# FFN raw tiles: four made and zeroed once per layer, instead of one GpSimd memset for each use

## The chip, the cores and the metric

The kernel runs on one core of one Trainium2 chip. The metric is device time in microseconds of one execution, as the median of several runs; lower is better. TensorE (PE in the profile) multiplies, VectorE (DVE), ScalarE (ACT) and GpSimd (POOL) do elementwise work, SyncE (SP) issues most transfers. PEld is the loading of weights into TensorE, which runs beside its matmuls.

## The reference, cut to what matters

Two layers, each a token mixer and then a gated convolutional FFN. The change lies in the FFN, which runs twice:

```
D_MODEL = 1024; SEQ = 1024; D_FF = 2816; FFN_CONV = 3

def causal_dwconv(x, w, b):
    k_width = w.shape[0]
    s = x.shape[1]
    xp = jnp.pad(x, ((0, 0), (k_width - 1, 0), (0, 0)))
    y = b
    for k in range(k_width):
        y = y + w[k] * xp[:, k:k + s]
    return y

def conv_ffn(xn, up_w, conv_w, conv_b, down_w):
    h = causal_dwconv(xn @ up_w, conv_w, conv_b)
    g, u = h[..., :D_FF], h[..., D_FF:]
    return (jax.nn.silu(g) * u) @ down_w
```

The convolution looks two tokens back, so each channel's sequence begins with zeros (`jnp.pad`).

## The kernel before, in words

Activations lie with channels on the 128 partitions and the 1024 tokens along the free axis, in two halves of 512. Every product is made in three passes on numbers that are split into a high part (a rounded copy, made by a cast on ScalarE) and a low part (what is left, made by a subtraction on GpSimd): high by high, high by low, low by high. So each weight block costs a cast `wh<-...` on ScalarE, then a subtraction `wl<-...` on GpSimd, and the third pass of each product cannot begin before that subtraction has ended.

`ffn_layer` makes 22 pairs of channel blocks (gate and value). Pairs 0 and 1 are made by plain products. Pairs 2 to 21 go through one loop (from line 968), an iteration each, which makes a 2 by 2 block product with seven half-size products in place of eight (a Winograd form), so that each iteration first needs sums of the weights: `sums` (lines 935 to 943, VectorE) writes the tiles `sa` and `sc` from the weight tiles `ws`. The products of an iteration are, in TensorE's order, `px` and `py` (weights from `ws`), `px` again and `pz` (from `sa`), `px` again (from `sc`, with the operand `t3h`), `pw` (from `a22h`), `pz` again (from `sc`): 84 matmuls of 512 columns. The third use of `px` adds on top of the second, after a ScalarE copy (line 979) has saved what stood there.

The results are gathered in raw tiles of 1028 columns: four columns in front, of which the last two are the zeros that the convolution looks back on, then the 1024 tokens. `new_raw` (lines 822 to 825) takes one from a pool of four buffers and zeroes the four columns on GpSimd. An iteration takes two (`lo` and `hi`), and `conv` (lines 834 to 847) reads them: on ScalarE the last tap (line 839), on VectorE the other two taps (line 841, two passes for each of the two tiles, four in a row), then the gate (silu, line 844, ScalarE), the product of gate and value (line 846, VectorE) and the store to `a_d`. The convolution of one iteration runs during the next one.

A layer of the language puts each engine's instructions into an order of its own and derives the waits; a buffer of a pool is given out again when the last reader of its old content is done. The memset of a buffer is therefore an instruction in GpSimd's queue that waits for VectorE. The functions that the change touches:

Of the kernel before, what the change touches and what calls it, by code (L numbers as in the profile page):

```python
# [9 lines left out]
F32 = mybir.dt.float32  # L10
# [8 lines left out]
P = 128  # L19
T = 1024  # L20
# [46 lines left out]
def trunk_kernel(ctx: ExitStack, tc: tile.TileContext, a: dict, stages=None):  # L67
    nc = tc.nc
    pe, act, dve, pool, sp = nc.tensor, nc.scalar, nc.vector, nc.gpsimd, nc.sync
# [733 lines left out]
    def ffn_layer(i, final_store, next_gain):  # L803
# [6 lines left out]
        sb = st.enter_context(tc.tile_pool(name=f"ffu{i}", bufs=2, reuse_waits="tile"))  # L810
# [8 lines left out]
        HB = KB // 2  # L819
        W2 = HB * P  # L820

        def new_raw():
            raw = sb.tile([P, T + 4], F32, name="raw", tag="raw", bufs=4)
            pool.memset(raw[:, 0:4], 0.0)
            return raw

        def half(raw, h):
            return raw[:, 4 + h * HT:4 + (h + 1) * HT]
# [53 lines left out]
        def load_pair(j):  # L882
# [6 lines left out]
            return {"ws": ws}  # L889

        raws = [new_raw() for _ in range(2 * PLAIN)]
        plain = [(h, n) for h in range(2) for n in range(2 * PLAIN)]
        w = split_weight(a["ffn_up_w"][i, 0], KB, 1)
# [73 lines left out]
        for j in range(PLAIN, PAIRS):  # L967
            end = j == PAIRS - 1
            nxt = None if end else load_pair(j + 1)
            lo, hi = new_raw(), new_raw()  # L970
            px, py = ps_a([P, HT], "px"), ps_b([P, HT], "py")
            pz, pw = (ups.tile([P, HT], F32, name=f"p{c}", tag=c) for c in "zw")
# [559 lines left out]
    for idx, s in enumerate(stages):  # L1532
        last = idx == len(stages) - 1
        ng = None if last else first_gain[stages[idx + 1]]
        if s == "ssd":
            ssd_layer(begin, ng if ng is not None else gffn[:, 0], prepare if "attn" in stages else (lambda: None))
        elif s in ("ffn0", "ffn1"):
            dst = a["out"] if last else x_d
            ffn_layer(int(s[-1]), dst, ng)
            src = dst  # L1540
        else:
            attn_layer(tabs["attn"], src, ng if ng is not None else gffn[:, 1])
        if last and not s.startswith("ffn"):
            for h in range(2):
                for m in range(KB):
                    store_x(a["out"], m, h)
# [87 lines left out]
```

## Time and profile before

| | |
|---|---|
| time, median of 3 runs | 2966.8 us (2965.51 to 2970.82) |
| the profiled execution: its own time | 2972.08 us |
| its span in the trace | 2970.4 us |
| TensorE busy | 2812.9 us, 95% of the span |
| VectorE busy | 2055.0 us, 69% |
| GpSimd busy | 1331.7 us, 45% |
| ScalarE busy | 1254.2 us, 42% |
| GpSimd memsets of line 824 | 88, of 101 ns each (median) |

Busy time of TensorE is what a step must shorten or uncover to matter; a busy or waiting GpSimd matters only where TensorE waits for it. Starts below are microseconds from the start of the span.

### The profile page before, as it was taken

Reading aid. Unit: us, or ns where it says so; the run is one execution under the profiler, and the core shown is the slowest. Engines: PE = TensorE matmul, PEld = TensorE weight load, DVE = VectorE, ACT = ScalarE, POOL = GpSimd, SP = SyncE. Lnnn points to the kernel's source line nnn. Section 1 sums busy time; section 2 is a strip of 40 time slices with the busy share of each in tenths; the row PEclk is TensorE's granted clock in tenths of the full one; section 3 lists DMA queues with packets and bytes.
Section 4 is the critical chain, followed back from the end, with each engine's and each line's share of the span. In section 5 each row is a group of like instructions: output and inputs, shape, how many; then the busy total and the mean of one; then the engine's idle time right before and its main releaser. Section 6 shows DMA issues by size and latency. Waiting matters only on the chain.

```text
span 2970.4 us, 36010 instructions
## 1 busy us (share of the span) xinstructions
PE 2812.9 (95%) x13156; PEld 2206.2 (74%) x13156; DVE 2055.0 (69%) x3160; ACT 1254.2 (42%) x2005; POOL 1331.7 (45%) x880
## 2 busy tenths in 40 slices
PE   6999999988998999999998999999999899999999
PEld 4877777767776888878876666666677688888887
DVE  5646574867778777773347888888868977777433
ACT  4434444443334444441124555555544444444211
POOL 3246564657456554542225433333436654453222
PEclk9999999999999999999999999999999999999999
DMA  3445454555432222233222212111444222224323
GB/s 102 139 133 168 151 167 154 170 186 175 152 121 100 86 85 86 77 126 131 96 99 87 53 58 60 58 58 50 143 138 135 104 82 82 86 85 152 110 87 112
DMA packets 182402, 329.93 MB, mean 111 GB/s; under 512 B 20369, under 2 KB 86929, under 8 KB 182225
## 3 DMA queue, kind: packets, MB, share of 16 engines
q1 hardware_dynamic: 154960, 253.16, 25.2%
q10 hardware_dynamic: 18432, 58.73, 5.8%
q0 software_dynamic: 8832, 15.73, 2.2%
q8 instruction: 104, 1.70, 0.2%
q14 instruction: 74, 0.60, 0.1%
HBM read 242.04 MB, written 77.14 MB: 107 GB/s over the span
## 4 chain that ended last, share of the span: by engine, by line
PE 63%; DVE 19%; DMA 5%; POOL 4%; ACT 4%; issue 4%; SPq 0%; ACTq 0%; POOLq 0%; DVEq 0%
PE px L949 10%; PE pz L949 7%; PE mm L302 6%; PE mm L304 5%; PE mm L303 5%; PE dp L122 5%; PE dp L123 5%; PE dp L121 5%; PE pw L949 3%; PE py L949 3%; PE s L1347 1%; DVE cv L450 1%; DVE cv L841 1%; PE s L1346 1%; POOL seg L583 1%
## 5 line engine op out<-in xcount | busy, mean ns | idle before, releaser
L108 POOL TENSOR_TENSOR wl<-ws,wh 128x1024 fp32r<-128x1024 f32 (+2 forms) x200 | 450.1, 2251 | 764.9 <-ACT wh L106 752.1
L302 PE MATMUL mm<-xh,wh 128*128 128x512 f32 x1280 | 539.3, 422 | 4.1 <-ACT xh L709 2.2
L303 PE MATMUL mm<-xl,wh 128*128 128x512 f32 x1280 | 508.9, 398 | 2.4 <-DVE xl L256 1.7
L304 PE MATMUL mm<-xh,wl 128*128 128x512 f32 x1280 | 507.5, 396 | 2.2 <-POOL wl L108 2.1
L106 ACT CAST wh<-ws 128x1024 fp32r<-128x1024 f32 (+2 forms) x200 | 191.1, 956 | 419.8 <-PE dp L122 227.1
L302 PEld LDWEIGHTS mm<-xh,wh 128*128 128x128 f32 x1280 | 245.1, 192 | 67.4 <-issue 17.4
L303 PEld LDWEIGHTS mm<-xl,wh 128*128 128x128 f32 x1280 | 244.9, 191 | 58.4 <-issue 8.3
L304 PEld LDWEIGHTS mm<-xh,wl 128*128 128x128 f32 x1280 | 244.0, 191 | 58.3 <-POOL wl L108 4.7
L1038 DVE TENSOR_TENSOR x<-x,dp 128x512 f32<-128x512 f32 x192 | 130.2, 684 | 213.9 <-PE dp L123 213.6
L122 PE MATMUL dp<-al,wh 128*128 128x512 f32 x704 | 274.9, 390 | 1.5 <-DVE al L832 1.5
L121 PE MATMUL dp<-ah,wh 128*128 128x512 f32 x704 | 275.1, 391 | 0.9 <-ACT ah L831 0.9
L123 PE MATMUL dp<-ah,wl 128*128 128x512 f32 x704 | 274.5, 390 | 0.0
L841 DVE SCALAR_TENSOR_TENSOR cv<-raw,fcw,cv 128x1024 f32<-128x1024 f32 x176 | 231.9, 1375 | 10.3 <-ACT cv L839 10.3
L450 DVE SCALAR_TENSOR_TENSOR cv<-raw,cw,cv 128x1024 f32<-128x1024 f32 x72 | 123.2, 1713 | 62.1 <-ACT cv L448 36.2
L122 PEld LDWEIGHTS dp<-al,wh 128*128 128x128 f32 x704 | 132.6, 188 | 29.7 <-DVE al L832 2.1
L121 PEld LDWEIGHTS dp<-ah,wh 128*128 128x128 f32 x704 | 132.4, 188 | 29.8 <-ACT ah L831 1.6
L123 PEld LDWEIGHTS dp<-ah,wl 128*128 128x128 f32 x704 | 132.6, 188 | 27.3
L1361 ACT ACTIVATE p<-s,nb,rq 128x256 f32<-128x256 f32 (+7 forms) x128 | 107.0, 836 | 106.7 <-DVE nb L1350 65.3
L876 POOL TENSOR_TENSOR wl<-sa,wh 128x1024 fp32r<-128x1024 f32 x40 | 96.2, 2404 | 82.3 <-ACT wh L876 82.3
L876 POOL TENSOR_TENSOR wl<-sc,wh 128x1024 fp32r<-128x1024 f32 x40 | 126.9, 3171 | 6.9 <-ACT wh L876 6.1
L876 POOL TENSOR_TENSOR wl<-ws,wh 128x1024 fp32r<-128x1024 f32 x40 | 108.8, 2720 | 31.0 <-ACT wh L876 31.0
L846 DVE TENSOR_TENSOR cv<-cv 128x1024 f32<-128x1024 f32 x44 | 115.7, 2630 | 0.3
(323 smaller groups left out, 6554.6 us busy)
## 6 DMA issues: line engine op xcount, KB each, us to landing
ws<-in_ffn_up_w_dram SPq DMA_DIRECT2D x96, 512.0 KB
a_d<-cv SPq DMA_DIRECT2D x44, 512.0 KB
ad<-a_d SPq DMA_DIRECT2D x44, 512.0 KB
ws<-in_ssd_in_w_dram ACTq DMA_DIRECT2D x40, 512.0 KB
seg<-acs_d SPq DMA_DIRECT2D x32, 512.0 KB
ws<-in_ssd_out_w_dram ACTq DMA_DIRECT2D x32, 512.0 KB
ws<-in_ffn_down_w_dram SPq DMA_DIRECT2D x32, 512.0 KB
xbc_d<-cv SPq DMA_DIRECT2D x24, 512.0 KB
```

The lines of the kernel that those rows point to most:

```text
L106: high = act.copy(wh[:, :n], ws[:, :n])
L108: last_split[0] = (high, pool.tensor_tensor(wl[:, :n], ws[:, :n], wh[:, :n], op=ALU.subtract))
L121: pe.matmul(ps, wh[:, m, k, :], xh, start=k == 0, stop=False)
L122: pe.matmul(ps, wh[:, m, k, :], xl, start=False, stop=False)
L123: pe.matmul(ps, wl[:, m, k, :], xh, start=False, stop=k == n - 1)
L302: pe.matmul(ps, wh[:, 0, k, :], xh, start=k == 0, stop=False)
L303: pe.matmul(ps, wh[:, 0, k, :], xl, start=False, stop=False)
L304: pe.matmul(ps, wl[:, 0, k, :], xh, start=False, stop=k == nk - 1)
L450: dve.scalar_tensor_tensor(cv, raw[:, 1 + k:1 + k + T], cw[:, i, k:k + 1], cv, op0=ALU.mult, op1=ALU.add)
L841: dve.scalar_tensor_tensor(cv, raws[b][:, 2 + k:2 + k + T], cw[:, n, k:k + 1], cv, op0=ALU.mult, op1=ALU.add)
L876: last_split[0] = (act.copy(wh, t), pool.tensor_tensor(wl, t, wh, op=ALU.subtract))
L949: pe.matmul(ps, l[:, k, :], r, start=first and k == 0 and n == 0, stop=k == HB - 1 and n == 2, skip_group_check=not first)
```

## The change

The four raw tiles are made under names of their own and zeroed at the layer's beginning. `new_raw` hands them out in turn and issues nothing. The columns 0 to 3 are never written again, so they stay zero.

```
+        raw_tiles = [sb.tile([P, T + 4], F32, name=f"raw{k}", tag=f"raw{k}", bufs=1) for k in range(4)]
+        for t in raw_tiles:
+            pool.memset(t[:, 0:4], 0.0)
+
         def new_raw():
-            raw = sb.tile([P, T + 4], F32, name="raw", tag="raw", bufs=4)
-            pool.memset(raw[:, 0:4], 0.0)
-            return raw
+            raw_tiles.append(raw_tiles.pop(0))
+            return raw_tiles[-1]
```

TensorE, ScalarE, VectorE and SyncE keep their order in every row. Only GpSimd's queue changes. There, before the change, one iteration of the FFN loop reads as follows (names: `wl` and `a22l` are low parts of weights, made from the tile named behind the arrow; the brackets name the engines and transfers waited for):

```order
L876 TENSOR_TENSOR a22l<-ws,a22h 128x512 [waits DMAHW3_49,PE_49,Activation_49]
L876 TENSOR_TENSOR wl<-sa,wh 128x1024 [waits PE_49,Activation_49]
L824 MEMSET raw 128x4 [waits DVE_49,Activation_49]
L876 TENSOR_TENSOR wl<-sc,wh 128x1024 [waits PE_49,Activation_49]
L824 MEMSET raw 128x4 [waits DVE_49]
L876 TENSOR_TENSOR wl<-ws,wh 128x1024 [waits DMAHW2_49,PE_49,Activation_49]
```

And with the change (its line 879 is line 876 of before):

```order
L879 TENSOR_TENSOR a22l<-ws,a22h 128x512 [waits DMAHW3_49,PE_49,Activation_49]
L879 TENSOR_TENSOR wl<-sa,wh 128x1024 [waits PE_49,Activation_49]
L879 TENSOR_TENSOR wl<-sc,wh 128x1024 [waits DVE_49,PE_49,Activation_49]
L879 TENSOR_TENSOR wl<-ws,wh 128x1024 [waits DMAHW2_49,PE_49,Activation_49]
L879 TENSOR_TENSOR a22l<-ws,a22h 128x512 [waits DMAHW0_49,PE_49,Activation_49]
```

The two memsets are gone, and `wl<-sc` now names VectorE itself: it reads `sc`, which line 942 wrote in the iteration before; until now the memset's wait had covered that.

At the loop's entrance GpSimd's queue before the change is this (`t1l`, `t3l`, `xl` are low parts of activations):

```order
L108 TENSOR_TENSOR wl<-ws,wh 128x1024 [waits DMAHW1_49,PE_49,Activation_49]
L824 MEMSET raw 128x4 [waits DVE_49]
L832 TENSOR_TENSOR t1l<-x_0_97,t1h 128x512 [waits Activation_49]
L832 TENSOR_TENSOR t3l<-x_1_105,t3h 128x512 [waits Activation_49]
L876 TENSOR_TENSOR wl<-ws,wh 128x1024 [waits DMAHW2_49,PE_49,Activation_49]
L824 MEMSET raw 128x4 [waits DVE_49]
L832 TENSOR_TENSOR xl_7057<-x_0_99,xh_7056 128x512 [waits Activation_49]
```

With the change it is:

```order
L108 TENSOR_TENSOR wl<-ws,wh 128x1024 [waits DMAHW1_49,PE_49,Activation_49]
L835 TENSOR_TENSOR t1l<-x_0_97,t1h 128x512 [waits DVE_49,Activation_49]
L835 TENSOR_TENSOR t3l<-x_1_105,t3h 128x512 [waits DVE_49,Activation_49]
L879 TENSOR_TENSOR wl<-ws,wh 128x1024 [waits DMAHW2_49,PE_49,Activation_49]
L835 TENSOR_TENSOR xl_7057<-x_0_99,xh_7056 128x512 [waits Activation_49]
```

Nothing but the memsets has left; their order among themselves is kept, and the four at the layer's very beginning stand where the first four stood.

## Rows read from the trace of the kernel before

**Rows 1.** Line 824's own view: idle before the memsets, then who waited (us, times).

```profile
  DVE cv L841: 167.9, 41
...
  PEld px L949: 19.9, 38
  PE px L949: 7.8, 3
```

**Rows 2.** Timeline of GpSimd, one iteration: start, us, instruction [idle before <-releaser].

```profile
1110.83 2.40 POOL L876 TENSOR_TENSOR wl<-sa,wh 128x1024 fp32r<-128x1024 f32 x1 [1.91 <-ACT wh L876]
1117.67 0.10 POOL L824 MEMSET raw<- 128x4 f32 x1 [4.44 <-DVE cv L841]
1117.79 3.23 POOL L876 TENSOR_TENSOR wl<-sc,wh 128x1024 fp32r<-128x1024 f32 x1
1120.95 0.09 POOL L824 MEMSET raw<- 128x4 f32 x1
```

**Rows 3.** Timeline of VectorE, the same iteration (the third convolution pass alone).

```profile
1109.89 0.69 DVE L1000 TENSOR_TENSOR raw<-raw,pz 128x512 f32<-128x512 f32 x1 [1.80 <-PE pz L949]
...
1116.27 1.28 DVE L841 SCALAR_TENSOR_TENSOR cv<-raw,fcw,cv 128x1024 f32<-128x1024 f32 x1
...
1119.26 2.83 DVE L846 TENSOR_TENSOR cv<-cv 128x1024 f32<-128x1024 f32 x1
```

**Rows 4.** Timeline of ScalarE, the same iteration.

```profile
1109.70 1.05 ACT L876 CAST wh<-sa 128x1024 fp32r<-128x1024 f32 x1 [2.14 <-PE pz L949]
...
1115.15 1.06 ACT L876 CAST wh<-sc 128x1024 fp32r<-128x1024 f32 x1 [1.64 <-PE py L949]
1117.58 1.06 ACT L844 ACTIVATE cv<-cv 128x1024 f32<-128x1024 f32 x1 [1.38 <-DVE cv L841]
1118.55 0.57 ACT L979 COPY raw<-px 128x512 f32<-128x512 f32 x1
```

**Rows 5.** Timeline of TensorE's matmuls, the same iteration.

```profile
1109.68 0.39 PE L949 MATMUL px<-xh,wh 128*128 128x512 f32 x1
...
1120.57 0.39 PE L949 MATMUL px<-t3h,wh 128*128 128x512 f32 x1
...
1121.63 0.40 PE L949 MATMUL px<-t3l,wh 128*128 128x512 f32 x1
```

**Rows 6.** Timeline of TensorE's weight loads: the first and the last such wait.

```profile
967.31 0.19 PEld L949 LDWEIGHTS px<-t3h,wl 128*128 128x128 f32 x1 [0.32 <-POOL raw L824]
...
2697.99 0.19 PEld L949 LDWEIGHTS px<-t3h,wl 128*128 128x128 f32 x1 [0.31 <-POOL raw L824]
```

**Rows 7.** Timelines of VectorE and GpSimd at two other places where both want to start.

```profile
900.04 0.68 DVE L832 TENSOR_TENSOR t3l<-x,t3h 128x512 fp32r<-128x512 f32 x1
...
900.00 2.95 POOL L108 TENSOR_TENSOR wl<-ws,wh 128x1024 fp32r<-128x1024 f32 x1 [2.84 <-ACT wh L106]
...
2352.73 1.27 DVE L841 SCALAR_TENSOR_TENSOR cv<-raw,fcw,cv 128x1024 f32<-128x1024 f32 x1
...
2353.92 3.42 DVE L841 SCALAR_TENSOR_TENSOR cv<-raw,fcw,cv 128x1024 f32<-128x1024 f32 x1
...
2352.81 3.45 POOL L876 TENSOR_TENSOR wl<-ws,wh 128x1024 fp32r<-128x1024 f32 x1 [2.96 <-ACT wh L876]
```

**Rows 8.** Timelines around the second iteration of the second FFN's loop.

```profile
2364.59 1.05 ACT L876 CAST wh<-sc 128x1024 fp32r<-128x1024 f32 x1
...
2366.41 1.28 DVE L841 SCALAR_TENSOR_TENSOR cv<-raw,fcw,cv 128x1024 f32<-128x1024 f32 x1
...
2370.50 0.39 PE L949 MATMUL px<-t3l,wh 128*128 128x512 f32 x1
2371.19 0.50 PE L949 MATMUL px<-t3h,wl 128*128 128x512 f32 x1 [0.31 <-POOL raw L824]
```

**Rows 9.** Timelines of GpSimd and TensorE at the entrance of the first FFN's loop.

```profile
923.15 1.88 POOL L832 TENSOR_TENSOR t1l<-x,t1h 128x512 fp32r<-128x512 f32 x1 [2.65 <-ACT t1h L831]
...
930.07 0.80 PE L949 MATMUL px<-xh,wl 128*128 128x512 f32 x1 [3.74 <-POOL raw L824]
```

## The prediction

> **What bounds the kernel now.** The page comes first: TensorE is busy 95% of the span, GpSimd 45%. So the memsets, 88 of 0.1 us on GpSimd, cost nothing by themselves; the question is whether TensorE waits for something that stands behind them. Line 824's own view answers who waits for whom [rows 1]: GpSimd stood 167.9 us in front of memsets, for the convolution's passes on VectorE (line 841), and TensorE's weight loads waited 38 times, 19.9 us, its matmuls 3 times, 7.8 us, for what the view calls the memset. No matmul reads a raw tile. What it reads is `wl`, and the timeline shows the mix-up: `wl<-sc` ends at 1117.79 + 3.23 = 1121.02, the second memset, queued right behind it, ends within 0.03 us of that, and the trace names the later of the two [rows 2].
>
> So I read one iteration, on four engines. The first memset may start when the third of the four convolution passes is through, at 1117.67; `wl<-sc` is queued behind it and starts at 1117.79 [rows 2]. Its cast had ended at 1115.15 + 1.06 = 1116.21 [rows 4], and a free GpSimd follows a cast 0.08 us later (1109.70 + 1.05 = 1110.75 against 1110.83) [rows 2, 4]. So the memset holds the subtraction back from 1116.29 to 1117.79, 1.5 us. On TensorE the first 48 matmuls of the iteration take 1120.57 - 1109.68 = 10.89 us, 0.227 each; the next four steps, in which the first `wl` of `sc` is wanted, take 1121.63 - 1120.57 = 1.06 instead of 0.91 [rows 5]. That is the whole loss: **0.15 us per iteration**. It stands alike in 35 iterations, 18 in the first FFN and 17 in the second, the first at 967.31 and the last at 2697.99 [rows 6].
>
> **The change part by part.** *What goes:* 80 of 88 memsets, 0.1 us each. At the loop's entrance and at every other place GpSimd has idle time around them, so I cost the instructions at nothing. The biggest waits that carry the memset's name are not the memset's: at 930.07 a matmul waits 3.74 us, but the `wl` that it wants is third behind `t1l`, which starts at 923.15 when ScalarE's cast releases it, long after the memset of that place [rows 9]. The second FFN has the same wait at the same place. Both stay: 0.
>
> *What is uncovered:* `wl<-sc` may now start at 1116.29, in the middle of the four convolution passes, and there it meets VectorE. The two engines do not run such passes side by side. In the trace a subtraction of this size takes 2.40 us when it is alone (1110.83) and 3.23 here, where it starts inside the fourth pass [rows 2]; line 846 takes 2.83 behind it [rows 3]. So I need to know who goes first. The third pass starts at 1116.27 [rows 3], 0.02 us ahead of GpSimd's new start. The nearest rows: at 2352.81 GpSimd came 0.08 us after a pass of the same line had begun (2352.73). It waited for that one pass and then ran: it ended at 2356.26, 3.53 after that pass's start, and the next pass, 2353.92, took 3.42 instead of 1.27 [rows 7]. At 900.00 GpSimd came 0.04 us *before* VectorE's next pass (900.04), which still went first: 0.68 for it, 2.95 for the subtraction [rows 7]. Eight places of the trace have VectorE's next start between 43 ns before and 49 ns after GpSimd's, with VectorE's previous pass still running; VectorE went first in all eight. From 134 ns on GpSimd went first. In the 35 iterations the third pass lies between 21 ns before and 9 ns after the point where GpSimd would start, so it goes first.
>
> Then `wl<-sc` runs between the third and the fourth pass and ends near 1116.27 + 3.53 = 1119.80, 1.2 us earlier than now. TensorE wants it about 1121.02 (1120.57 + 2 x 0.227). The wait goes: 35 x 0.15 = **-5.3 us**. What is late next? The fourth pass, by 3.42 - 1.27 = 2.15 us, so line 846, which now waits for the subtraction until 1121.02 and ends at 1122.09, ends some 0.6 later. Behind it on VectorE stand the weight sums and the additions from PSUM, then line 1000, which has 1.80 us of idle in front of it, waiting for TensorE [rows 3]. That covers 0.6; without cover it would cost 0.6 per iteration. The silu and the copy of line 979, which TensorE needs, follow the third pass, which keeps its time.
>
> *The exception:* in the second iteration of the second FFN the cast ends at 2364.59 + 1.05, so GpSimd would come at 2365.72, 0.7 us ahead of the third pass (2366.41) [rows 8]. By the rows above GpSimd goes first and that pass ends 2.15 late. Line 979 ends 2.85 us after the third pass's start (1118.55 + 0.57 - 1116.27) [rows 3, 4], hence at 2366.41 + 2.85 + 2.15 = 2371.41, and TensorE, which wanted to go on at 2370.27 (one step before 2370.50), waits 1.2 us. Today it loses 2371.19 - 2370.50 - 0.23 = 0.46 there [rows 8]. **+0.7 us.**
>
> *Sum:* -5.3 + 0.7 = -4.6 us. The profiled execution took 2972.08, 5.3 over the median of the three runs shown; its own time would become 2967.5, and the median 2966.8 - 4.6 = **2962.2 us**, 0.16% less. I take 0.2%, 5.9 us, as the least that a measurement of this kernel can tell from no change: its three runs span 5.3 us.
>
> **A rule of the skill.** Above, VectorE goes first even where it starts up to 49 ns later [rows 7]. The Trainium skill, "SBUF — State Buffer", section "SBUF: two separate sides", says that the port pair which VectorE (with two SBUF inputs) and GpSimd share is an exclusive lock, and that whichever *starts* first has it for the whole instruction. The trace agrees on the lock, 3.42 against 1.27; on who is first by start it does not, at 900.00. Taken to the letter the rule gives the second rival below.
>
> **The rivals.** *Slower: GpSimd slips in ahead of the third pass in every iteration.* Then the silu, which waits for that pass (1117.58), and the copy behind it in ScalarE's queue are 2.15 late [rows 4]; line 979 ends at 1119.12 + 2.15 = 1121.27, and TensorE, free at 1120.57, goes on 0.05 later: 0.75 us of waiting and 0.1 to get going again, less the 0.15 saved, +0.7 per iteration. 35 x 0.7 + 0.7 = +25.2: 2992 us. For it: the margin is some tens of nanoseconds. Against it: the eight places. It decides from the point where GpSimd arrives about 50 to 130 ns ahead of the third pass. Chance 0.09.
>
> *A mixture by order of start.* In 5 of the 35 iterations GpSimd's new start comes first, by 1 to 9 ns. If it then wins: 30 x -0.15 + 5 x 0.7 + 0.7 = -0.3, 2966.5 us. Chance 0.08. The rule cited above would have it so.
>
> *No change: VectorE keeps all four passes.* If GpSimd is let in only after the fourth, `wl<-sc` ends at 1121.02 as now and nothing is gained: 2966.8 us. The 3.42 at 2353.92 speaks against it. Chance 0.07.
>
> *The view at face value.* If all 19.9 + 7.8 = 27.7 us named after the memset were TensorE time and went [rows 1]: 2939 us. Against it: a weight load's wait of 0.31 costs TensorE 0.15, since loads run ahead of the matmuls, and the two long waits have another cause [rows 5, 6, 9]. Chance 0.03.
>
> **How the numbers follow.** The forecast has 0.70; 0.03 is left for what I have not seen. Within the forecast the time may lie between 2959 and 2965, by the spread of the runs and by 0.15 us being a difference of rounded starts: about a quarter of it is beyond 5.9 us. Faster by over 0.2%: 0.17 + 0.03 + a little of the rest, 0.22. Slower: the first rival and a part of the rest, 0.11. Same: 0.67. The range for 8 in 10 takes in the forecast, the mixture and no change: 2957 to 2969 us; the first rival and the face value lie outside it.
>
> **What the changed profile would show.** GpSimd's `wl<-sc` starting 0.08 us after its cast, taking about 3.5 us and ending 1.0 us before TensorE's `px<-t3h,wl`; one pass in four of line 841 at about 3.4 us, and it the last; no wait of `px<-t3h,wl` for GpSimd; 52 steps from an iteration's first matmul in 11.8 us instead of 11.95; line 979 at its old place. I am wrong if the third pass is the long one, if line 979 ends later and TensorE waits for ScalarE at `px<-t3h,wh`, if line 1000 becomes late, or if the entrance of the loops takes another course than today.

## The result: slower by half a per cent, a mixture of both orders

The changed kernel takes 2987.27 us (median of 10 runs) where the kernel before took 2970.96: a ratio of 1.0051, 95% interval 1.0039 to 1.0064. The ratios here and below are the record's own and not quotients of the medians beside them. One execution of an experiment below, pass_silu_late, took 3792 us at a granted clock of 0.669 and is left out of its ratio. The forecast was 2962.2 us, with 2957 to 2969 as its range; the time lies above it, 25 us from the forecast. The profiled execution of the changed kernel took 2985.59 us, with a span of 2983.9 against 2970.4 before: 13.5 us more.

All lines behind the insertion have moved down by 3: line 844 holds the convolution's passes (841 before), 847 the silu (844), 879 the split of a weight (876), 952 the products (949), 982 the copy that TensorE needs (979), 1003 the last addition (1000).

The first view is that of line 982, the ScalarE copy that stands behind the silu.

```profile
L982 ACT COPY raw<-px x40: 562/567/587, 946.4 to 2729.8; 128x512 f32<-128x512 f32 x40
...
  PEld px L952: 17.1, 16
  PE px L952: 10.3, 16
```

And the same copy before (its line 979), where the list of those who waited for it is empty; the waits of the steady iterations carried the memset's name [rows 1, 6].

```profile
L979 ACT COPY raw<-px x40: 562/567/591, 945.2 to 2715.7; 128x512 f32<-128x512 f32 x40
...
who waited for it (us, times):
busy tenths in 40 slices 0000000000000000000000000000000000000000
```

So 16 times TensorE now waits for this copy, 0.64 us each. The iteration of before that stands in the rows runs from 1109.68 [rows 5] to the next one's first matmul, 19.22 us later:

```profile
1128.90 0.39 PE L949 MATMUL px<-xh,wh 128*128 128x512 f32 x1
```

The loops have 36 steady iterations (18 in each FFN). Next two neighbouring iterations in the timelines of the four engines; the first runs from 1054.80 to 1073.84, the second from there to 1093.85.

```profile
1054.80 0.39 PE L952 MATMUL px<-xh,wh 128*128 128x512 f32 x1
...
1060.26 1.06 ACT L879 CAST wh<-sc 128x1024 fp32r<-128x1024 f32 x1 [1.64 <-PE py L952]
...
1061.38 1.28 DVE L844 SCALAR_TENSOR_TENSOR cv<-raw,fcw,cv 128x1024 f32<-128x1024 f32 x1
...
1061.40 3.51 POOL L879 TENSOR_TENSOR wl<-sc,wh 128x1024 fp32r<-128x1024 f32 x1 [3.06 <-ACT wh L879]
...
1062.57 3.42 DVE L844 SCALAR_TENSOR_TENSOR cv<-raw,fcw,cv 128x1024 f32<-128x1024 f32 x1
...
1062.68 1.06 ACT L847 ACTIVATE cv<-cv 128x1024 f32<-128x1024 f32 x1 [1.36 <-DVE cv L844]
1063.65 0.57 ACT L982 COPY raw<-px 128x512 f32<-128x512 f32 x1
...
1065.67 0.39 PE L952 MATMUL px<-t3h,wh 128*128 128x512 f32 x1
...
1073.84 0.39 PE L952 MATMUL px<-xh,wh 128*128 128x512 f32 x1
...
1074.04 0.69 DVE L1003 TENSOR_TENSOR raw<-raw,pz 128x512 f32<-128x512 f32 x1 [1.10 <-PE pz L952]
...
1080.42 3.47 DVE L844 SCALAR_TENSOR_TENSOR cv<-raw,fcw,cv 128x1024 f32<-128x1024 f32 x1
...
1080.43 2.38 POOL L879 TENSOR_TENSOR wl<-sc,wh 128x1024 fp32r<-128x1024 f32 x1 [3.04 <-ACT wh L879]
...
1083.82 1.27 DVE L844 SCALAR_TENSOR_TENSOR cv<-raw,fcw,cv 128x1024 f32<-128x1024 f32 x1
...
1083.93 1.06 ACT L847 ACTIVATE cv<-cv 128x1024 f32<-128x1024 f32 x1 [3.58 <-DVE cv L844]
1084.89 0.56 ACT L982 COPY raw<-px 128x512 f32<-128x512 f32 x1
...
1085.51 0.50 PE L952 MATMUL px<-t3h,wh 128*128 128x512 f32 x1 [0.64 <-ACT raw L982]
...
1093.85 0.39 PE L952 MATMUL px<-xh,wh 128*128 128x512 f32 x1
```

Read the two `wl<-sc` rows against the pass next to them. In the first iteration it starts 0.02 us behind the third pass and waits for it: the third pass takes 1.28 us, the subtraction ends at 1061.40 + 3.51 = 1064.91, the fourth pass takes 3.42, and TensorE goes on without a wait. The period is 1073.84 - 1054.80 = 19.04 us, 84 matmuls of 0.227 with no gap left; before it was 19.22. This is the course that the prediction described, line 1003 included, which still has 1.10 us of idle in front of it (1.80 before, [rows 3]). In the second iteration the subtraction starts 0.01 us behind the third pass and yet runs at once, 2.38 us, while that pass takes 3.47. The silu waits for it until 1083.93, the copy of line 982 ends at 1085.45, and TensorE waits. The period is 1093.85 - 1073.84 = 20.01.

There is no third kind. In this trace 20 steady iterations have VectorE first (19.04 us) and 16 have GpSimd first (19.97 to 20.03). Of the 35 that stood at 19.22 before, 20 gain 0.18 and 15 lose some 0.77: +8.0 us, and by the first matmuls of the iterations these 35 did grow by 5.25 in the first loop and 2.64 in the second, 7.9 together. The rest of the 13.5 lies elsewhere. The first iteration of each loop is 1.0 and 2.9 us longer; 1.6 is spread over the parts outside. For the second FFN's first iteration the table of stretches of the two kernels shows why (after its length come the engines' busy times, the granted clock of TensorE, DMA share and GB/s), first of the changed kernel:

```profile
2343.93:2370.45 26.52, 23.25 (x82) 18.14 (x81) 22.59 (x19) 9.55 (x12) 15.68 (x8) 0.82 0.48 167
```

and of the kernel before:

```profile
2335.51:2359.12 23.61, 21.47 (x82) 16.89 (x81) 20.59 (x17) 9.03 (x12) 15.03 (x9) 0.89 0.51 178
```

TensorE has the same matmuls and a lower granted clock. Both stretches begin with matmuls that start 0.427 us apart, which is the 1.2 GHz level, and go on at 0.227, the 2.4 GHz level. The longer one falls back to 0.427 once more, 13 times, behind waits of 2.05 and 1.22 us; the shorter one stays at 0.227 behind waits of 0.92 and 1.22. These 13 make 2.6 of the 2.9 us. Whether the change brings this about is a question for the experiments.

### The profile page after: what moved, and what is told of

It is laid out like the page before. It is cut to its first block, busy times and chain, and to the rows that moved or that the text cites. A ratio compares the mean times of both kernels' runs of the same rounds, so it can differ in the third digit from the quotient of the medians.

```text
span 2983.9 us, 35900 instructions
## 1 busy us (share of the span) xinstructions
PE 2813.4 (94%) x13156; PEld 2211.4 (74%) x13156; DVE 2077.0 (70%) x3160; ACT 1252.4 (42%) x2005; POOL 1326.0 (44%) x800
## 4 chain that ended last, share of the span: by engine, by line
PE 65%; DVE 19%; ACT 5%; DMA 4%; POOL 4%; issue 4%; SPq 0%; ACTq 0%; DVEq 0%; POOLq 0%
PE px L952 11%; PE pz L952 7%; PE mm L302 6%; PE mm L304 6%; PE mm L303 6%; PE dp L122 5%; PE dp L123 5%; PE dp L121 5%; PE pw L952 3%; PE py L952 3%; DVE cv L450 2%; PE s L1350 1%; PE s L1349 1%; DVE nb L1353 1%; PE pv L1412 1%
## 5 line engine op out<-in xcount | busy, mean ns | idle before, releaser
L844 DVE SCALAR_TENSOR_TENSOR cv<-raw,fcw,cv 128x1024 f32<-128x1024 f32 x176 | 310.0, 1818 | 11.5 <-ACT cv L842 11.5
L879 POOL TENSOR_TENSOR wl<-sc,wh 128x1024 fp32r<-128x1024 f32 x40 | 119.9, 2997 | 115.6 <-ACT wh L879 115.6
L879 POOL TENSOR_TENSOR wl<-ws,wh 128x1024 fp32r<-128x1024 f32 x40 | 116.9, 2923 | 108.2 <-ACT wh L879 108.2
L943 DVE TENSOR_TENSOR sa<-sa,ws 128x512 f32<-128x512 f32 x40 | 109.6, 2741 | 0.0
```

Of the source, the lines that this page charges most:

```text
L844: dve.scalar_tensor_tensor(cv, raws[b][:, 2 + k:2 + k + T], cw[:, n, k:k + 1], cv, op0=ALU.mult, op1=ALU.add)
L879: last_split[0] = (act.copy(wh, t), pool.tensor_tensor(wl, t, wh, op=ALU.subtract))
```

## The experiments

**The theories.** *Theory L (lock order):* the loss is that of the iterations in which GpSimd gets in ahead of the third pass, by way of the silu and the copy of line 982. *Rival C (clock):* the loss is TensorE's half-speed stretch at the loops' entrances. *Rival M:* every iteration pays something for the memset that is missing. *Rival D:* TensorE is late by the fourth pass and what follows it on VectorE, not by the silu. Each kernel was timed in five rounds against the kernel before on the same chip. All edits are to the changed kernel unless said otherwise. The expectations count 37 steady iterations; there are 36.

**after_again**: no edit.

> The changed kernel once more, nothing edited. Theory L (lock order): GpSimd's wl<-sc and VectorE's third convolution pass ask for the same thing within some 20 ns, and who is first differs from iteration to iteration; where GpSimd is first the third pass is 2.2 us late, the silu and the copy of line 982 behind it too, and TensorE waits. It expects both kinds of iteration again (19.04 us where VectorE is first, 19.97 to 20.03 where GpSimd is), no third kind, and 8 to 24 iterations with GpSimd first, not all the same ones; a time 0.3 to 0.7% above before. Rival C (clock): the lost time is mainly TensorE's half-speed stretch in the first iteration of each loop (3.9 us longer in the profile after); it expects these stretches again with the same length, and a time that goes with them. Rival M (missing memset): every iteration pays something for the absent memset, so iterations would differ little.

Measured: 2981.81 us against 2974.39, ratio 1.0029 (1.0019 to 1.0038). Again 16 of 36 iterations have GpSimd first, but others: 6 in the first FFN and 10 in the second, against 9 and 7. The periods are 19.04 and 19.99 to 20.03. Rival M is out, since most iterations are faster than before. The ratio of the first measurement was higher, so the size of the loss is not a fixed number.

**lo_memset**: one of the two memsets put back, that which stood ahead of `wl<-sc`.

```
             lo, hi = new_raw(), new_raw()
+            pool.memset(lo[:, 0:4], 0.0)
```

> The changed kernel with one memset per iteration put back, that of the lo tile alone, which stands ahead of wl<-sc in GpSimd's queue and must wait for the third pass. Theory L: wl<-sc starts after the third pass again, in every iteration, so all periods are 19.2 us again and the time is that of before within 0.2% (16 us below the changed kernel). Rival C: the time stays at that of the changed kernel, 0.5% above before. Rival M: half of the loss is back, some 8 us.

Measured: 2973.34 against 2974.39, ratio 0.9999 (0.999 to 1.0007). The timeline of GpSimd has the old picture:

```profile
1065.35 0.10 POOL L974 MEMSET raw<- 128x4 f32 x1 [4.38 <-DVE cv L844]
1065.44 3.30 POOL L879 TENSOR_TENSOR wl<-sc,wh 128x1024 fp32r<-128x1024 f32 x1
```

All periods are 19.21 to 19.26. The stretch of the second FFN's first iteration in this kernel's trace:

```profile
2343.10:2369.60 26.50, 23.19 (x82) 18.13 (x81) 22.59 (x19) 9.55 (x12) 15.76 (x9) 0.82 0.51 167
```

It is the long one at the low clock, in a kernel whose median is that of before. The traced execution took 2981.51 us, 8 over that median, so by itself it does not say what the long stretch costs the others. But tt_third, below, has the long one as well (26.40 us), in an execution of 2968.0 us, 3 us under the median of before. So the long first iteration is not what makes the changed kernel slower: rival C is out. One memset of 0.10 us per iteration decides the whole difference between the medians.

**hi_memset**: the other memset put back, which stands behind `wl<-sc`.

```
             lo, hi = new_raw(), new_raw()
+            pool.memset(hi[:, 0:4], 0.0)
```

> The changed kernel with one memset per iteration put back, that of the hi tile alone, which stands behind wl<-sc in GpSimd's queue. Theory L: wl<-sc is free as in the changed kernel, so both kinds of iteration occur again, about 16 of 37 with the third pass at 3.4 us, and the time is 0.2 to 0.6% above before. Rival: the memset behind wl<-sc matters too, and the time is between that of before and of the changed kernel.

Measured: 2977.79 against 2971.69, ratio 1.0017 (1.0007 to 1.0027), 12 of 36 iterations with GpSimd first, periods 19.04 and 19.97 to 20.03. It is a mixture as in the changed kernel, with a loss just under the 0.2% expected. That it is a little faster than the changed kernel goes with 12 in place of 16, but one trace of each does not show whether the memset changes that share.

**cast_late**: GpSimd made to come later.

```
+            if late:
+                act.copy(wh[:, 0:128], t[:, 0:128])
             last_split[0] = (act.copy(wh, t), ...
...
-            cur["a3"] = split(cur["sc"])
+            cur["a3"] = split(cur["sc"], late=True)
```

> The changed kernel with a small ScalarE cast (128x128, into the same wh tile) ahead of the cast of sc, so that GpSimd's wl<-sc comes 0.1 to 0.3 us later, clearly behind the start of the third pass. Theory L: VectorE is first in every iteration, every steady period 19.04 us against 19.22 before: 37 x 0.18 = 6.7 us below before, about 2964 where before is 2971. Rival C and rival M: no change against the changed kernel, 0.5% above before.

Measured: 2972.76 against 2974.39, ratio 0.9997 (0.9989 to 1.0006). GpSimd now starts 0.38 to 0.41 us after the third pass (0.11 in one iteration), VectorE is first in all 36, and all periods are 19.04: the mechanism is as expected, the time is not, 5 us short. The timeline of ScalarE in a loop's last iteration shows what went wrong, and that of TensorE what it cost:

```profile
1304.14 0.30 ACT L880 CAST wh<-sc 128x128 fp32r<-128x128 f32 x1 [1.64 <-PE py L954]
1304.35 1.05 ACT L834 CAST ah<-ad 128x1024 fp32r<-128x1024 f32 x1
1305.73 1.06 ACT L847 ACTIVATE cv<-cv 128x1024 f32<-128x1024 f32 x1 [0.34 <-DVE cv L844]
1306.70 1.04 ACT L881 CAST wh<-sc 128x1024 fp32r<-128x1024 f32 x1
...
1313.15 0.68 PE L954 MATMUL px<-t3h,wl 128*128 128x512 f32 x1 [2.98 <-POOL wl L881]
```

There the real cast had slipped behind another cast and the silu; TensorE waited 3 us, in each of the two loops.

**cast_late2**: the same without the last iteration (`late=not end`).

> As cast_late, without the small cast in each loop's last iteration, where it had pushed the cast of sc behind the silu (a 3.4 us wait of TensorE twice). Theory L: VectorE first in all 37 steady iterations, periods 19.04 us, and the last iterations as in the changed kernel: 6 us below before, about 0.2%. Rival C: the clock of the entrances decides and the time stays within 0.1% of before.

Measured: 2964.2 against 2971.33, ratio 0.998 (0.9969 to 0.9991): 7 us below before, 6 expected. 35 of 36 periods are 19.04; the first one of the second FFN is 20.65, and there GpSimd came 0.30 us ahead of the third pass, against the expectation.

**pass_late**: the third pass made to come later. Not shown here and in pass_late3: the second of the weight sums on VectorE is held behind the last pass.

```
                 for k in range(2):
                     dve.scalar_tensor_tensor(cv, ...)
+                    if b == 0 and k == 0:
+                        dve.tensor_copy(cv[:, 0:64], cv[:, 0:64])
```

> The changed kernel with a small VectorE copy (128x64, in place) between the second and the third pass, so that the third pass comes about 0.1 to 0.2 us after GpSimd's wl<-sc. Theory L: GpSimd is first in every steady iteration, all periods 20.0 us: 37 x 0.78 = 29 us above before, about 3000 where before is 2971. Rival C and rival M: 0.5% above before, as the changed kernel, or a microsecond or two more for the added copies (44 x 0.06).

Measured: 3074.01 against 2974.39, ratio 1.0337, over three times the loss expected; periods of 21.2 and 22.85. GpSimd was first in every iteration, but the edit had done more: the gate tile's second pass had changed places with the other tile's, so the silu waited for the fourth pass and not the third. That is a mistake of the experiment; it shows only that TensorE follows the silu.

**pass_late3**: the order held.

```
+                    with behind(passes[-1:] if (b, k) == (1, 1) and j >= PLAIN else []):
                         p = dve.scalar_tensor_tensor(cv, ...)
+                    if (b, k) == (0, 0) and j >= PLAIN:
+                        dve.tensor_copy(cv[:, 0:64], cv[:, 0:64])
```

> As pass_late, but with the gate tile's second pass held ahead of the other tile's (in pass_late the copy had changed places between them, so that the silu waited for the fourth pass), and the copy in the steady iterations alone. Theory L: GpSimd is first in every steady iteration by some 0.1 us, the third pass takes 3.4 us, the silu starts behind it, TensorE waits about 1.1 us at px<-t3h,wh and all steady periods are about 20.1 us: 37 x 0.8 to 0.9 = 30 to 34 us above before. A rival (P): the third pass is not what TensorE waits through, and the 2.3 us gaps of pass_late come from the added copies; then periods stay at 21 to 23 us, 90 us above before.

Measured: 3003.72 against 2971.33, ratio 1.0121 (1.0106 to 1.0137): +32 us, all steady periods 20.01 to 20.07. From the view of waits and the timelines:

```profile
PE px L959 <- ACT raw L989: 25.0, 36, 0.7
```

```profile
1049.74 2.43 POOL L885 TENSOR_TENSOR wl<-sc,wh 128x1024 fp32r<-128x1024 f32 x1 [3.04 <-ACT wh L885]
...
1049.95 3.30 DVE L847 SCALAR_TENSOR_TENSOR cv<-raw,fcw,cv 128x1024 f32<-128x1024 f32 x1
...
1053.29 1.06 ACT L853 ACTIVATE cv<-cv 128x1024 f32<-128x1024 f32 x1 [3.62 <-DVE cv L847]
1054.25 0.57 ACT L989 COPY raw<-px 128x512 f32<-128x512 f32 x1
...
1054.87 0.50 PE L959 MATMUL px<-t3h,wh 128*128 128x512 f32 x1 [0.69 <-ACT raw L989]
```

The 16 waits of the changed kernel have become 36. This is the first rival of the prediction, forced: it gave +25 us (2992) for 35 iterations at +0.7, and +32 came.

**silu_late**: the silu queued behind the copy of line 982, the product and its store behind the silu.

```
+            def finish(snap):
+                with behind([snap] if snap else []):
+                    act.activation(cvs[0], cvs[0], AF.Silu)
+                dve.tensor_tensor(cvs[1], cvs[0], cvs[1], op=ALU.mult)
+                sp.dma_start(a_d[j], cvs[1])
+            return finish
...
             snap = act.copy(half(lo, 1), px)
+            if fin:
+                fin.pop()(snap)
```

> The changed kernel with the silu queued behind the copy of line 982 on ScalarE (and the product of the two tiles and its store behind it); nothing else is moved. Theory L: both orders of GpSimd and VectorE go on to occur, the third pass is again 3.4 us in part of the iterations, but TensorE no longer waits, since the copy that it needs stands ahead of the silu: all steady periods 19.04 us, about 0.2% below before. A rival (D): TensorE's wait comes by the late fourth pass, line 849 and the additions from PSUM and not by the silu; then iterations with GpSimd first stay at 20 us and the time at 0.3 to 0.5% above before.

Measured: 2964.25 against 2971.33, ratio 0.9976 (0.9963 to 0.9989). In 15 of the 36 steady iterations the third pass is still the long one, and 34 periods are 19.04 (the first two of the second FFN 19.26 and 19.18). The timeline of an iteration with GpSimd first:

```profile
1229.65 2.39 POOL L882 TENSOR_TENSOR wl<-sc,wh 128x1024 fp32r<-128x1024 f32 x1 [3.04 <-ACT wh L882]
...
1229.64 3.48 DVE L844 SCALAR_TENSOR_TENSOR cv<-raw,fcw,cv 128x1024 f32<-128x1024 f32 x1
...
1231.41 0.59 ACT L986 COPY raw<-px 128x512 f32<-128x512 f32 x1 [1.84 <-PE px L955]
1233.16 1.07 ACT L850 ACTIVATE cv<-cv 128x1024 f32<-128x1024 f32 x1 [1.16 <-DVE cv L844]
...
1233.93 0.39 PE L955 MATMUL px<-t3h,wh 128*128 128x512 f32 x1
```

The pass is as late as in the changed kernel, the copy (line 986 here) is through before the silu starts, and TensorE does not wait. Rival D is out.

**pass_silu_late**: pass_late3 and silu_late together.

> pass_late3 and silu_late together: GpSimd first in every iteration, the silu behind the copy of line 982. Theory L: periods 19.04 us although every third pass takes 3.4 us, about 0.2% below before. Rival D: periods about 20 us, 1% above before.

Measured: 2965.72 against 2971.33, ratio 0.9973 (0.9961 to 0.9984). GpSimd ahead of the third pass in all but one of the 36, where neither waits, and steady periods of 19.04 (one of 19.13, the first of the second FFN 19.24). The move of the silu takes 38 us off pass_late3.

**before_silu_late**: the same move in the kernel before, memsets kept.

> The kernel before, with its 88 memsets, and only the silu moved behind the copy of line 979 (the move of silu_late alone, without the change). Theory L: the memset still holds wl<-sc until the third pass is through, so the steady periods stay at 19.2 us and the time is within 0.1% of before; the 0.24% of silu_late then belong to the two edits together. Rival S: the silu's place is worth the gain by itself, whatever the memsets do; then periods of 19.04 us and 0.2% below before.

Measured: 2971.13 against 2971.69, ratio 1.0001 (0.9989 to 1.0012), periods of 19.23 and 19.26. The move alone gains nothing, the change alone loses, both together gain 0.24%. This kernel too had a long first iteration in the second FFN, 26.44 us.

**tt_third**: why did the eight places mislead? The third pass alone made a plain addition; the kernel leaves out that pass's coefficient.

```
+                    if (b, k) == (0, 1):
+                        dve.tensor_tensor(cv, raws[b][:, 3:3 + T], cv, op=ALU.add)
+                        continue
                     dve.scalar_tensor_tensor(cv, ...)
```

> The changed kernel with the third pass alone as a plain addition of two tensors (TENSOR_TENSOR, like the eight places that the prediction took its rule from) in place of the scaled one (SCALAR_TENSOR_TENSOR): it leaves out that pass's coefficient, reads and writes the same tiles and stands at the same place. In the traces so far plain two-tensor instructions on VectorE went first when they started up to 49 ns after GpSimd and GpSimd from 49 to 50 ns on, while the scaled third pass lost from 5 ns ahead of GpSimd on and won from 10 ns ahead. Theory F (form): the boundary belongs to the form of VectorE's instruction; with the third pass at -25 to +10 ns against GpSimd, VectorE is first in all 36 steady iterations, periods 19.04 us, and the time about 6 us (0.2%) below before. Rival W (place): at this place GpSimd wins the same share whatever the form, some 12 to 16 of 36 iterations at 20 us, 0.15 to 0.5% above before.

Measured: 2967.12 against 2970.98, ratio 0.9984 (0.997 to 0.9997). VectorE is first in all 36, with the pass starting between 21 ns ahead of GpSimd and 7 ns behind it, and all periods are 19.04. The timelines where it came behind:

```profile
1097.17 3.49 POOL L882 TENSOR_TENSOR wl<-sc,wh 128x1024 fp32r<-128x1024 f32 x1 [3.03 <-ACT wh L882]
...
1097.17 1.22 DVE L845 TENSOR_TENSOR cv<-raw,cv 128x1024 f32<-128x1024 f32 x1
...
1098.31 3.43 DVE L847 SCALAR_TENSOR_TENSOR cv<-raw,fcw,cv 128x1024 f32<-128x1024 f32 x1
```

At the same place and the same nanoseconds the plain form goes first where the scaled form lost: theory F, and not rival W.

## Why the prediction was wrong

**The reading of before was right.** The memset held `wl<-sc` back and cost TensorE time in each iteration; the estimate was 0.15 us, it is 19.22 - 19.04 = 0.18. `wl<-sc` starts 0.08 us after its cast, and where VectorE is first the course is the predicted one to a tenth of a microsecond, with line 1003's idle covering the late fourth pass. lo_memset shows that this memset is what held it.

**The step that failed** is "In the 35 iterations the third pass lies between 21 ns before and 9 ns after the point where GpSimd would start, so it goes first." Its rule came from eight places where VectorE went first though it started up to 49 ns after GpSimd [rows 7]. All eight are plain TENSOR_TENSOR instructions; the third pass is a SCALAR_TENSOR_TENSOR. Its boundary lies elsewhere, and the trace of before had places that show it, which the count of eight leaves out. A scaled instruction of line 1350, of one column, starts 17 to 38 ns after a GpSimd instruction six times while VectorE's previous pass still runs. GpSimd went first in all six: the scaled one took 1.25 to 1.27 us each time, to GpSimd's end, where the median of its 128 is 0.158. One of them:

```profile
1671.74 1.25 DVE L1350 SCALAR_TENSOR_TENSOR nb<-nb,rq 128x1 f32<-128x1 f32 x1
...
1671.71 1.26 POOL L1194 TENSOR_TENSOR qg<-qg,rk 128x512 f32<-128x512 f32 x1
```

For the third pass itself, I set 143 of them against `wl<-sc` in four traces (after, after_again, hi_memset, silu_late): 62 of 62 that started 10 ns or more ahead of GpSimd went first; of 38 that started 6 to 9 ns ahead, 23 did; of 43 that started at most 5 ns ahead, or behind, none did. The boundary of the scaled form is thus near -7 ns, that of the plain form near +49. tt_third shows that the form makes the difference. The rows of before, held against the right boundary, would have given 7 of the 35 iterations to GpSimd and left 6 to chance, with GpSimd 78 ns behind its cast, and 12 and 3 with 77 ns, the delay of most rows in the changed kernel: a loss of a few microseconds either way. The changed kernel has 15 of them.

**The rivals.** What came is the mixture by order of start, forecast at 5 of 35 iterations and 2966.5 us, with a chance of 0.08. Its mechanism held, and so did the price of an iteration with GpSimd first: +0.7 was worked out, 0.75 to 0.81 came. Only the count was too low. The rule that was set aside there, that whoever starts first has the port pair (the Trainium skill, "SBUF — State Buffer", section "SBUF: two separate sides"), comes within 10 ns for the scaled form and misses by 49 ns for the plain one. The first rival's mechanism came when pass_late3 forced it, at 0.8 us per iteration where 0.7 was worked out.

**The exception** in the second FFN's second iteration was costed at +0.7 us. It grew by 0.07 (19.91 to 19.99): its first iteration took another course, the long one, and it became an ordinary iteration with GpSimd first.

**The entrances.** "Both stay: 0" held for the two long waits. The first iterations were nevertheless 1.0 and 2.9 us longer in the profiled execution. In after_again the first loop's was as in before (25.2 us). For the second, lo_memset and before_silu_late had the long one with the memset in place, cast_late2 and silu_late the short one (23.6 us) without it, so it is not the change's. The record names the chip of the experiments, though not of the first measurement: all seven traces from chip 4 have a long one (26.2 to 26.5 us), and three of the four from chip 5 the short one (pass_late3 25.1). What decides between the two is not settled.

**What stays open.** The steady iterations explain 7.9 of the profile's 13.5 us, and about half of the 16 us between the medians. The rest was not taken apart: the ratios of the two measurements of the same kernel, 1.0051 and 1.0029, differ by more than their intervals, and there is one profile of each. In after_again the steady iterations are 8.0 us longer than those of before, by the two traces, which covers the whole 7.4 us between its medians; what is left over stands in the first measurement and not in this one.

## What to carry to other kernels

A wait that looks useless can be what keeps two engines in a good order. Before taking it away, look at what the freed instruction meets, and if two engines then ask for the same thing within some tens of nanoseconds, plan for both orders and price the worse one, or make the order harmless: here one ScalarE instruction moved behind another turned a loss of 0.3 to 0.5% into a gain of 0.24%. When a rule on who goes first is read off other places of a trace, those places must have the same form of instruction, not only the same engines.

## What the runs showed of the hardware

Where both want to start while VectorE's previous pass still runs, who goes first depends on the form of VectorE's instruction. By VectorE's start against GpSimd's, the boundary lies near -7 ns for SCALAR_TENSOR_TENSOR, and near +49 ns for TENSOR_TENSOR (the plain subtraction `t3l<-x,t3h` of [rows 7] went first at +47 and +49 ns in the trace of before, and second at +49 in that of cast_late2 and at +50 in that of silu_late). Between -6 and -9 ns the scaled form goes either way, so that the same program had GpSimd first in 16 iterations twice, but not in the same ones. The pass that loses is 2.1 to 2.2 us longer, the subtraction that loses 1.1 us (3.51 against 2.38).
